# A two-layer hybrid decoder trunk on one core: side work placed by other costs, norm steps and groups of products in another order, the last norm on VectorE

## The chip, the core and the metric

The kernel runs on one core of a Trainium2 chip. Times are device microseconds of one execution, from the launch of the program on the core to its end; the metric is the median of the timed runs. TensorE multiplies matrices, VectorE, ScalarE and GpSimd work elementwise and by rows, and SyncE's queue issues most transfers.

## What is computed

For 256 tokens of width 1024 a norm, and then two layers, each of which is

```python
h = LN(ALPHA * h + mixer(h))          # ALPHA = 4 ** 0.25
h = LN(ALPHA * h + (silu(conv(gate)) * val) @ w_down)    # gate, val = split(h @ w_up)
```

The mixer projects h by one matrix into the inputs of three branches. Branch A is forgetting attention (a cumulated log gate added to the logits). Branch B is sparse attention: an indexer gives each key a score, the 64 best are kept by a top-k search, and attention runs over those. Branch C is differential attention, softmax1 - lambda * softmax2, normed per head. Queries and keys of B, C and the indexer are rotated by position. Each branch goes through its own matrix, is multiplied by a sigmoid gate of h, and the sum is projected once more.

## The kernel before

**Tiling.** The tokens are two blocks of 128 (tb 0 and 1). A norm's result h[tb][q] has 128 tokens and half of the width (q 0 and 1; the trace and the order call both "h", the order also h_90 to h_93 for h[0][0], h[0][1], h[1][0], h[1][1]). fp32 operands are split into a high and a low part, and each product is three matmuls (mm3): high by high, low by high, high by low. hTh and hTl are the transposed halves of h, which transposes on TensorE (with ident), a copy on ScalarE (hTh) and a subtraction on VectorE (hTl) make.

**Weights.** Class Stream reads all weights once, in chunks of two items of 512 columns (332 in the unit g1), by SyncE's queue into seven raw buffers. Each item is split: ScalarE copies the high half of an hl tile and VectorE (GpSimd for three items at the start) subtracts the low half. There are 16 hl buffers, so that the items split and not yet used are a reserve for TensorE. A layer has 292 items.

**The order.** The program is emitted in one sequence, and each engine works its own rows in that order. What sets the order is a planner: class Clocks keeps a clock per engine by modelled durations (cost, L195) and the time at which a tile is done. A unit of products calls Tasks.tick after every mm3; tick moves the side tasks on (generators: rotation task_rope_T, the indexer and top-k task_index, attention task_A, task_B, task_C, the merge of the branches, the MLP's activation) and calls Stream.refill, which emits a split when fewer than LOW = 3 items are in reserve, or when VectorE's clock is less than BEHIND = 1000 ns ahead of TensorE's and W.hold isn't set. A side task waits in ready (L361) until its inputs are done by these clocks. T.until ticks with idle time until a condition holds.

**Norms.** Between the halves of a layer the last products come piece by piece: for each block two halves nh of 512 columns, after each of which ln_half (L486) adds the product to h and takes its statistics; ln_tail (L545) is added as a side task, with the norm (ln_apply, L502: for each half of the width the subtraction of the mean times the gain lng, then the factor rs plus the bias lnb; rs itself is a power on GpSimd), the transposes and the splits into hTh and hTl. The next unit (unit_x_tbfirst, L573, at a layer's start, the loop of up0, L1106, in the MLP) multiplies block 0 by all its eight weight items first, and then block 1, as soon as a block's transposes are emitted (its flag). W.hold stops spare splits from the beginning of the last pieces until both tails are emitted.

**The end.** The last norm has two forms: block 0's (last_norm0, L520) by ScalarE, with gain and bias on GpSimd for one half and on VectorE for the other, and block 1's (last_norm1, L512) on VectorE; four stores of 256 KB.

## Time and profile before

| | us |
|---|---|
| timed runs | 935.35, 933.64, 935.29 (median 935.29) |
| the profiled execution's own time | 933.45 |
| its span, first to last instruction | 931.7 |
| TensorE busy | 900.1 (97%) |
| VectorE busy | 655.7 (70%) |
| ScalarE busy | 513.1 (55%) |
| GpSimd busy | 47.0 (5%) |

Every emitted instruction has the line of one helper, L242, so the profile is read by tiles and by time, not by lines. The timeline shows instructions one after the other, those alike merged (x4), with the idle time of the engine ahead of them and what ended it, in brackets. The ends of matmuls are modelled: a matmul of 512 columns shows 0.39 us, but the next begins 0.23 after it (0.12 for 256 columns); idle time that the view shows is therefore a little less than what a wait costs. The granted clock is TensorE's, 1.00 is full speed (2.4 GHz) and 0.5 half of it.

### The profile page before, as it was taken

Reading aid. Unit: us, or ns where it says so; the run is one execution under the profiler, and the core shown is the slowest. Engines: PE = TensorE matmul, PEld = TensorE weight load, DVE = VectorE, ACT = ScalarE, POOL = GpSimd, SP = SyncE. Lnnn points to the kernel's source line nnn. Section 1 sums busy time; section 2 is a strip of 40 time slices with the busy share of each in tenths; the row PEclk is TensorE's granted clock in tenths of the full one; section 3 lists DMA queues with packets and bytes.
Section 4 is the critical chain, followed back from the end, with each engine's and each line's share of the span. In section 5 each row is a group of like instructions: output and inputs, shape, how many; then the busy total and the mean of one; then the engine's idle time right before and its main releaser. Section 6 shows DMA issues by size and latency. Waiting matters only on the chain.

```text
span 931.7 us, 14406 instructions
## 1 busy us (share of the span) xinstructions
PE 900.1 (97%) x5306; PEld 787.9 (85%) x5306; DVE 655.7 (70%) x1270; ACT 513.1 (55%) x1008; POOL 47.0 (5%) x62
## 2 busy tenths in 40 slices
PE   4999999999999999999999999999999999999995
PEld 3877887888878999999888788888888799999994
DVE  7888686566678766756688957765667886766755
ACT  4753776655537655555466456765554375655540
POOL 5000010011000000000000001000110100000001
PEclk9999999999999999999999999999999999999998
DMA  8843166566526765565355322936565286566601
GB/s 307 276 141 114 48 220 236 177 200 192 189 96 227 235 196 187 181 195 182 105 185 168 113 89 72 353 115 204 186 201 176 85 295 195 178 195 188 182 3 45
DMA packets 46535, 161.45 MB, mean 173 GB/s; under 512 B 5696, under 2 KB 6208, under 8 KB 46464
## 3 DMA queue, kind: packets, MB, share of 16 engines
q1 hardware_dynamic: 44208, 154.94, 51.1%
q0 software_dynamic: 1408, 4.98, 1.6%
q8 instruction: 41, 0.67, 0.3%
q10 hardware_dynamic: 848, 0.60, 0.2%
q14 instruction: 30, 0.25, 0.1%
HBM read 159.46 MB, written 1.05 MB: 172 GB/s over the span
## 4 chain that ended last, share of the span: by engine, by line
PE 84%; DVE 9%; issue 3%; ACT 2%; DMA 1%; POOL 1%; SPq 0%; DVEq 0%; POOLq 0%; ACTq 0%
PE acc L242 52%; PE att L242 32%; DVE h L242 2%; DVE s L242 1%; DVE hl L242 1%; DVE a L242 1%; POOL rs L242 1%; DMA raw<-in_w_dram 1%; ACT a L242 1%; ACT p L242 1%; DMA lnb<-in_ln_in_b_dram 1%; DVE bst L242 1%; DVE smx L242 0%; ACT hl L242 0%; DVE t L242 0%
## 5 line engine op out<-in xcount | busy, mean ns | idle before, releaser
L242 DVE TENSOR_TENSOR hl<-raw,hl 128x512 fp32r<-128x512 f32 (+1 forms) x581 | 389.3, 695 | 185.5 <-ACT hl L242 183.9
L242 ACT ACTIVATE hl<-raw 128x512 fp32r<-128x512 f32 (+1 forms) x584 | 347.7, 624 | 192.8 <-PE att L242 92.4
L242 PE MATMUL acc<-hl,hTh 128*128 128x512 f32 (+1 forms) x896 | 285.7, 391 | 3.2 <-DVE hl L242 2.0
L242 PE MATMUL att<-hTh,hl 128*128 128x256 f32 x1280 | 231.3, 283 | 0.0
L242 PEld LDWEIGHTS att<-hTh,hl 128*128 128x128 f32 x1280 | 200.8, 192 | 1.4
L242 PEld LDWEIGHTS acc<-hl,hTh 128*128 128x128 f32 x896 | 168.3, 189 | 38.1 <-DVE hl L242 2.7
L242 PE MATMUL att<-hTl,hl 128*128 128x256 f32 x640 | 181.1, 283 | 0.0
L242 PE MATMUL acc<-hl,hTl 128*128 128x512 f32 (+1 forms) x448 | 173.4, 387 | 1.8 <-DVE hTl L242 1.8
L242 PE MATMUL acc<-hl,act 128*128 128x512 f32 x528 | 123.4, 390 | 0.0
L242 PEld LDWEIGHTS att<-hTl,hl 128*128 128x128 f32 x640 | 122.8, 192 | 0.0
L242 PEld LDWEIGHTS acc<-hl,act 128*128 128x128 f32 x528 | 97.9, 188 | 19.5
L242 PEld LDWEIGHTS acc<-hl,hTl 128*128 128x128 f32 x448 | 85.0, 190 | 17.8 <-DVE hTl L242 2.7
L242 PE MATMUL acc<-hl,oT 128*128 128x512 f32 x288 | 68.0, 391 | 0.0
L242 PEld LDWEIGHTS acc<-hl,oT 128*128 128x128 f32 x288 | 53.8, 188 | 11.0
L242 PE MATMUL acc<-hTh,hl 128*128 128x256 f32 x256 | 48.4, 289 | 3.5 <-DVE hl L242 3.5
L242 DVE SCALAR_TENSOR_TENSOR cv<-att,convp,cv 128x255 f32<-128x255 f32 x88 | 40.4, 480 | 15.4 <-ACT cv L242 13.9
L242 PE MATMUL acc<-hl,mT 128*128 128x512 f32 x192 | 45.5, 392 | 0.0
L242 PEld LDWEIGHTS acc<-hTh,hl 128*128 128x128 f32 x256 | 40.3, 192 | 5.2 <-DVE hl L242 3.9
L242 ACT ACTIVATE hTh<-att 128x512 fp32r<-128x512 f32 x16 | 9.6, 599 | 58.6 <-PE att L242 58.6
L242 PEld LDWEIGHTS acc<-hl,mT 128*128 128x128 f32 x192 | 35.6, 188 | 7.1
L242 PE MATMUL acc<-hTl,hl 128*128 128x256 f32 x128 | 36.4, 284 | 0.0
L242 POOL TENSOR_TENSOR rs<-mv,mhalf 128x1 f32<-128x1 f32 x10 | 9.1, 906 | 482.4 <-DVE mv L242 482.2
(161 smaller groups left out, 686.5 us busy)
## 6 DMA issues: line engine op xcount, KB each, us to landing
raw<-in_w_dram SPq DMA_DIRECT2D x284, 512.0 KB, 4.2
raw<-in_w_dram SPq DMA_DIRECT2D x8, 332.0 KB, 4.2
lng<-in_ln_g_dram POOLq DMA_DIRECT2D x4, 512.0 KB, 4.1
lnb<-in_ln_b_dram POOLq DMA_DIRECT2D x4, 512.0 KB, 6.4
h<-in_x_dram SPq DMA_DIRECT2D x4, 256.0 KB, 4.8
lng<-in_ln_in_g_dram SPq DMA_DIRECT2D x2, 256.0 KB, 4.9
lnb<-in_ln_in_b_dram SPq DMA_DIRECT2D x2, 256.0 KB, 5.3
wu<-in_w_ukv_dram POOLq DMA_DIRECT2D x2, 256.0 KB, 3.1
```

Of the source, the lines that this page charges most:

```text
L242: f(*args, **kw)
```

## The change

1. The planner's modelled durations are other ones, for VectorE, ScalarE's copy of an accumulated sum, table loads and GpSimd; what another engine than TensorE makes counts as done 230 ns after it, not 150, and a tile that the engine made itself isn't waited for.
2. ready also holds a side task back while the clock of its engine is more than LAG = 2500 ns ahead of TensorE's, and, on VectorE and in the projections from g1 to av, while fewer than three items are in reserve.
3. ln_apply does both subtractions and then both scalings.
4. unit_x_tbfirst and up0 take four weight items at a time (mm3_group): four matmuls high by high, four low by high, four high by low.
5. Between the halves of a layer, the last ln_half of block 1 moves into ln_tail, behind block 0's flag.
6. W.hold is set one piece later, so that one more split is emitted ahead of each norm.
7. In layer 1 the table load of ScalarE comes behind the first unit, not ahead of it.
8. The last norm is one form for both blocks, on VectorE alone, with stores of 512, 256 and 256 columns by the queues of SyncE, ScalarE and SyncE.

```diff
+LAG = 2500.0
...
-            if op == "reciprocal":
-                return 60 + 8 * n
+            if op in ("reciprocal", "bn_aggr"):
+                return 155 if op == "reciprocal" else 210
             if op == "match_replace":
-                return 140 + 1.05 * n
-            return 60 + n * (0.53 if op in ("tensor_copy", "tensor_scalar") else 1.05)
+                return 130 + 1.05 * n
+            if op == "scalar_tensor_tensor":
+                return 110 + 1.2 * n
+            if op in ("tensor_reduce", "max", "bn_stats"):
+                return 95 + 1.08 * n
+            if op == "tensor_scalar" or (op == "tensor_copy" and args[1].name[:3] not in ("att", "acc")):
+                return 150 + 0.5 * n
+            return max(160, 125 + 0.93 * n)
         if eng == "ACT":
             return 75 + 0.85 * n
-        return 630 if n <= 16 else 100 + 2.2 * n
+        return 900 if n <= 8 else 250 if n <= 32 else 100 + 2.2 * n
...
+        if op == "preload_act_table_set":
+            self.clk[eng] += 1280
+            self.table = "exp"
...
-        start = max([self.clk[eng]] + [self.done.get(x.name, 0) for x in aps[1:]])
+        start = max([self.clk[eng]] + [self.done.get(x.name, 0) for x in aps[1:] if self.by.get(x.name) != eng])
         self.clk[eng] = start + self.cost(eng, op, out, aps)
+        if "accum_out" in kw:
+            self.clk[eng] += 155
+        if eng == "ACT" and len(args) > 2 and args[2] in TABLES and TABLES[args[2]] != self.table:
+            self.table = TABLES[args[2]]
+            self.clk[eng] += 1280
         for o in outs:
-            self.done[o] = self.clk[eng] + 150
+            self.done[o] = self.clk[eng] + (150 if eng == "PE" else 230)
+            self.by[o] = eng
...
     def ready(eng, *aps):
-        while any(clocks.done.get(x.name, 0) > clocks.now(eng) - MARGIN.get(eng, 0) for x in aps):
+
+        while (any(clocks.done.get(x.name, 0) > clocks.now(eng) - MARGIN.get(eng, 0) for x in aps)
+               or clocks.clk[eng] > clocks.clk["PE"] + LAG
+               or (eng == "DVE" and l_now[0] and W.next_split - W.used < 3)):
...
     def ln_apply(tb, st, g, b):
         mu, rs = ln_stats(st)
         for q in range(2):
-            y, gq, bq = h[tb][q], g[:, 512 * q:512 * q + 512], b[:, 512 * q:512 * q + 512]
-            ve.scalar_tensor_tensor(y, y, mu, gq, ALU.subtract, ALU.mult)
-            ve.scalar_tensor_tensor(y, y, rs, bq, ALU.mult, ALU.add)
-    def store(tb, q):
-        (nc.sync, sc)[q].dma_start(out[0, tb * P:(tb + 1) * P, 512 * q:512 * q + 512], h[tb][q])
-    def last_norm1(st, g, b):
+            ve.scalar_tensor_tensor(h[tb][q], h[tb][q], mu, g[:, 512 * q:512 * q + 512], ALU.subtract, ALU.mult)
+        for q in range(2):
+            ve.scalar_tensor_tensor(h[tb][q], h[tb][q], rs, b[:, 512 * q:512 * q + 512], ALU.mult, ALU.add)
+    def last_norm(tb, st, g, b):
         mu, rs = ln_stats(st)
         for q in range(2):
-            ve.scalar_tensor_tensor(h[1][q], h[1][q], mu, g[:, 512 * q:512 * q + 512], ALU.subtract, ALU.mult)
-        for q in range(2):
-            ve.scalar_tensor_tensor(h[1][q], h[1][q], rs, b[:, 512 * q:512 * q + 512], ALU.mult, ALU.add)
-            store(1, q)
-    def last_norm0(st, g, b, half_done):
-        mu, rs = ln_stats(st)
-        nmr = small([P, 1], "nmr")
-        ve.scalar_tensor_tensor(nmr, mu, -1.0, rs, ALU.mult, ALU.mult)
-        for q in range(2):
-            sc.activation(h[0][q], h[0][q], AF.Identity, bias=nmr, scale=rs)
-        gp.tensor_tensor(h[0][0], h[0][0], g[:, 0:512], ALU.mult)
-        gp.tensor_tensor(h[0][0], h[0][0], b[:, 0:512], ALU.add)
-        while not half_done:
-            yield
-        ve.tensor_tensor(h[0][1], h[0][1], g[:, 512:1024], ALU.mult)
-        ve.tensor_tensor(h[0][1], h[0][1], b[:, 512:1024], ALU.add)
-        store(0, 1)
-        yield from ready("POOL", h[0][0])
-        nc.sync.dma_start(out[0, 0:P, 0:512], h[0][0])
+            ve.scalar_tensor_tensor(h[tb][q], h[tb][q], mu, g[:, 512 * q:512 * q + 512], ALU.subtract, ALU.mult)
+        for i, (c0, c1) in enumerate(((0, 512), (512, 768), (768, 1024))):
+            y = h[tb][c0 // 512][:, c0 % 512:c0 % 512 + c1 - c0]
+            ve.scalar_tensor_tensor(y, y, rs, b[:, c0:c1], ALU.mult, ALU.add)
+            (nc.sync, sc, nc.sync)[i].dma_start(out[0, tb * P:(tb + 1) * P, c0:c1], y)
...
-    def ln_tail(tb, st, hT, g, b, flag):
+    def ln_tail(tb, st, hT, g, b, flag, bank=None):
+        if bank is not None:
+            while 0 not in flag:
+                yield
+            ln_half(tb, 1, st, bank)
         ln_apply(tb, st, g, b)
...
+    def mm3_group(o, ls, ws, first, last):
+        n = len(ls)
+        for i, (lh, ll) in enumerate(ls):
+            mm(o, lh, ws[i][0], first and i == 0, False)
+        T.tick()
+        for i, (lh, ll) in enumerate(ls):
+            mm(o, ll, ws[i][0], False, False)
+        T.tick()
+        for i, (lh, ll) in enumerate(ls):
+            mm(o, lh, ws[i][1], False, last and i == n - 1)
+            if i % 2:
+                T.tick()
...
-            for k in range(kts):
+            for k in range(0, kts, 4):
                 if tb == 0:
-                    ws.append(W.take())
-                lh, ll = lhs(k, tb)
-                mm3(bk[tb][:, :ncols], lh, ll, ws[k][:, 0, :ncols], ws[k][:, 1, :ncols], k == 0, k == kts - 1)
+                    ws += [W.take() for _ in range(4)]
+                mm3_group(bk[tb][:, :ncols], [lhs(i, tb) for i in range(k, k + 4)],
+                          [(w[:, 0, :ncols], w[:, 1, :ncols]) for w in ws[k:k + 4]], k == 0, k + 4 == kts)
                 if tb == 1:
-                    W.free()
-                T.tick()
+                    W.free(4)
...
+        bk = unit_x_tbfirst(lhs, KD, 512, hflag)
         if l:
             sc.preload_act_table_set("natural_log_exp_and_others")
-        bk = unit_x_tbfirst(lhs, KD, 512, hflag)
         T.add(task_rope_T(evac(bk), 4, 32, 128 ** -0.5, "qbT"))
         bk = unit_x(lhs, KD, NG1)
+        l_now[0] = 1
...
+        l_now[0] = 0
...
-        W.hold = True
         hT1, flag1 = new_hT(), set()
         for tb in range(2):
             ts = slice(tb * P, (tb + 1) * P)
             st = small([P, 2, 6], "bst")
             for i, (nh, c0, c1) in enumerate(PIECES):
+                W.hold = W.hold or nh == 1
...
-                ln_half(tb, nh, st, ob[nh][tb], (c0, c1), i)
-            T.add(ln_tail(tb, st, hT1, lng, lnb, flag1))
+                if not (tb and nh):
+                    ln_half(tb, nh, st, ob[nh][tb], (c0, c1), i)
+            T.add(ln_tail(tb, st, hT1, lng, lnb, flag1, ob[1][1] if tb else None))
...
```

The order of the up0 loop is changed like that of unit_x_tbfirst, and the down projection's tail like the out projection's; the last layer calls last_norm for both blocks.

VectorE, at the norm between attention and MLP of layer 0, end of block 1 (h_92, h_93; rs is the norm's factor; an hl row is a split of the next unit's weights). Before:

```order
L242 SCALAR_TENSOR_TENSOR h_92<-h_92,mv_2753,lng_1683 128x512
L242 SCALAR_TENSOR_TENSOR h_92<-h_92,rs_2756,lnb_1684 128x512
L242 SCALAR_TENSOR_TENSOR h_93<-h_93,mv_2753,lng_1683 128x512
L242 SCALAR_TENSOR_TENSOR h_93<-h_93,rs_2756,lnb_1684 128x512
L242 TENSOR_TENSOR hl_2774<-raw_2488,hl_2774 128x512
L242 TENSOR_TENSOR hTl_2667<-att_2782,hTh_2666 128x4x128
L242 TENSOR_TENSOR hl_2789<-raw_2521,hl_2789 128x512
L242 TENSOR_TENSOR hTl_2667<-att_2795,hTh_2666 128x4x128
L242 TENSOR_TENSOR hl_2802<-raw_2521,hl_2802 128x512
```

After:

```order
L261 SCALAR_TENSOR_TENSOR h_92<-h_92,mv_2759,lng_1672 128x512
L261 SCALAR_TENSOR_TENSOR h_93<-h_93,mv_2759,lng_1672 128x512
L261 SCALAR_TENSOR_TENSOR h_92<-h_92,rs_2762,lnb_1673 128x512
L261 SCALAR_TENSOR_TENSOR h_93<-h_93,rs_2762,lnb_1673 128x512
L261 TENSOR_TENSOR hl_2780<-raw_2521,hl_2780 128x512
L261 TENSOR_TENSOR hl_2787<-raw_2521,hl_2787 128x512
L261 TENSOR_TENSOR hl_2794<-raw_2540,hl_2794 128x512
L261 TENSOR_TENSOR hTl_2667<-att_2799,hTh_2666 128x4x128
L261 TENSOR_TENSOR hTl_2667<-att_2806,hTh_2666 128x4x128
L261 TENSOR_TENSOR hl_2820<-raw_2540,hl_2820 128x512
```

Both scalings now stand behind both subtractions, and three splits stand ahead of both hTl, where one stood ahead of each.

TensorE, in the same place, from the last transposes of block 0 (h_91) into up0. Before:

```order
L242 MATMUL att_2740<-ident,h_91 128x128 x4
L242 MATMUL acc_2749<-hl_2592,hTh_2666 128x512
L242 MATMUL acc_2749<-hl_2592,hTl_2667 128x512
L242 MATMUL acc_2749<-hl_2592,hTh_2666 128x512
L242 MATMUL acc_2749<-hl_2603,hTh_2666 128x512
```

After:

```order
L261 MATMUL att_2745<-ident,h_91 128x128 x4
L261 MATMUL acc_2752<-hl_2589,hTh_2666 128x512
L261 MATMUL acc_2752<-hl_2600,hTh_2666 128x512
L261 MATMUL acc_2752<-hl_2620,hTh_2666 128x512
L261 MATMUL acc_2752<-hl_2629,hTh_2666 128x512
L261 MATMUL acc_2752<-hl_2589,hTl_2667 128x512
L261 MATMUL acc_2752<-hl_2600,hTl_2667 128x512
```

The first row that needs hTl was the second behind the transposes and is now the fifth.

VectorE, layer 1, end of the differential attention's softmax (smx a row's maximum, rina and rinv its factors; the eight SCALAR_TENSOR_TENSOR rows a<-p combine the two maps; hl rows are splits). Before:

```order
L242 RECIPROCAL rina_5675<-ssm_5753 128x2
L242 TENSOR_SCALAR a_427_5673<-a_427_5673,rina_5675 128x256 x2
L242 RECIPROCAL rinv_5676<-ssm_5758 128x2
L242 RECIPROCAL rina_5675<-ssm_5771 128x2
L242 TENSOR_SCALAR a_427_5673<-a_427_5673,rina_5675 128x256 x2
L242 RECIPROCAL rinv_5676<-ssm_5776 128x2
L242 TENSOR_SCALAR rinv_5676<-rinv_5676,nlam 128x8
L242 SCALAR_TENSOR_TENSOR a_425_5671<-p_426_5672,rinv_5676,a_425_5671 128x128 x4
L242 SCALAR_TENSOR_TENSOR a_427_5673<-p_428_5674,rinv_5676,a_427_5673 128x256 x4
L242 TENSOR_TENSOR hl_5814<-raw_5336,hl_5814 128x512
L242 TENSOR_TENSOR hl_5831<-raw_5367,hl_5831 128x512
L242 TENSOR_TENSOR hl_5846<-raw_5367,hl_5846 128x512
```

After:

```order
L261 TENSOR_TENSOR hl_5828<-raw_5427,hl_5828 128x512
L261 TENSOR_TENSOR hl_5845<-raw_5461,hl_5845 128x512
L261 RECIPROCAL rina_5667<-ssm_5804 128x2
L261 TENSOR_SCALAR a_427_5665<-a_427_5665,rina_5667 128x256 x2
L261 TENSOR_TENSOR hl_5868<-raw_5461,hl_5868 128x512
L261 TENSOR_REDUCE smx_5879<-att_5764 128x2
L261 TENSOR_TENSOR hl_5890<-raw_5529,hl_5890 128x512
L261 TENSOR_TENSOR hl_5905<-raw_5529,hl_5905 128x512
L261 RECIPROCAL rinv_5668<-ssm_5881 128x2
L261 TENSOR_SCALAR rinv_5668<-rinv_5668,nlam 128x8
L261 SCALAR_TENSOR_TENSOR a_425_5663<-p_426_5664,rinv_5668,a_425_5663 128x128 x4
L261 SCALAR_TENSOR_TENSOR a_427_5665<-p_428_5666,rinv_5668,a_427_5665 128x256 x4
```

Before, no split stands between the softmax steps; after, five do in this piece (and three more among the softmax rows ahead of it), and the eight steps stand behind them.

VectorE, the end of the program (nmr is used by ScalarE's form of the norm). Before:

```order
L242 SCALAR_TENSOR_TENSOR nmr_9229<-mv_9224,rs_9227 128x1
L242 SCALAR_TENSOR_TENSOR h_92<-h_92,acc_7577 128x512
L242 BN_STATS bst_9220<-h_92 128x6
L242 TENSOR_TENSOR h_91<-h_91,lng_7404 128x512
L242 TENSOR_TENSOR h_91<-h_91,lnb_7405 128x512
L242 SCALAR_TENSOR_TENSOR h_93<-h_93,acc_7579 128x512
L242 BN_STATS bst_9220<-h_93 128x6
```

After:

```order
L261 SCALAR_TENSOR_TENSOR h_90<-h_90,mv_9220,lng_7404 128x512
L261 SCALAR_TENSOR_TENSOR h_91<-h_91,mv_9220,lng_7404 128x512
L261 SCALAR_TENSOR_TENSOR h_90<-h_90,rs_9223,lnb_7405 128x512
L261 SCALAR_TENSOR_TENSOR h_91<-h_91,rs_9223,lnb_7405 128x256 x2
L261 SCALAR_TENSOR_TENSOR h_92<-h_92,acc_7574 128x512
L261 BN_STATS bst_9233<-h_92 128x6
L261 SCALAR_TENSOR_TENSOR h_93<-h_93,acc_7576 128x512
L261 BN_STATS bst_9233<-h_93 128x6
```

Block 0's norm is now five steps of one kind (two subtractions, three scalings), all of them ahead of block 1's first sum (h_92 with acc).

## Rows read from the trace of the kernel before

**Rows 1.** The page: busy time of each engine, its share of the span, instructions.

```profile
PE 900.1 (97%) x5306; PEld 787.9 (85%) x5306; DVE 655.7 (70%) x1270; ACT 513.1 (55%) x1008; POOL 47.0 (5%) x62
```

**Rows 2.** TensorE by stretch: length, busy (instructions), granted clock, DMA share, GB/s.

```profile
24.00:520.00 496.00, 490.62 (x2893) 1.00 0.55 178
...
571.00:574.40 3.40, 3.40 (x18) 0.50 0.78 227
```

**Rows 3.** TensorE's waits by what ended them: us in total, times, longest.

```profile
PE acc L242 <- DVE hl L242: 5.4, 3, 2.0
PE att L242 <- DVE t L242: 3.0, 3, 1.4
```

**Rows 4.** Timeline, TensorE, start: at, length, instruction [idle before, what ended it].

```profile
8.53 1.11 PE L242 MATMUL att<-ident,h 128*128 128x128 f32 x4 [8.53 <-DMA lnb<-in_ln_in_b_dram]
...
22.51 0.50 PE L242 MATMUL acc<-hl,hTh 128*128 128x512 f32 x1 [1.96 <-DVE hl L242]
```

**Rows 5.** Timeline, VectorE, start: norm of block 1 and item 6.

```profile
17.61 1.76 DVE L242 SCALAR_TENSOR_TENSOR h<-h,rs,lnb 128x512 f32<-128x512 f32 x1 [0.47 <-POOL rs L242]
...
21.76 0.70 DVE L242 TENSOR_TENSOR hl<-raw,hl 128x512 fp32r<-128x512 f32 x1
```

**Rows 6.** Timeline, GpSimd, the same stretch.

```profile
17.54 2.97 POOL L242 TENSOR_TENSOR hl<-raw,hl 128x512 fp32r<-128x512 f32 x2
```

**Rows 7.** Timeline, TensorE, layer 0: three waits in the projections.

```profile
52.79 0.41 PE L242 MATMUL att<-ident,t 128*128 128x128 f32 x2 [0.40 <-DVE t L242]
...
72.90 0.74 PE L242 MATMUL att<-ident,t 128*128 128x128 f32 x5 [1.39 <-DVE t L242]
...
119.66 0.38 PE L242 MATMUL acc<-hTh,hl 128*128 128x256 f32 x1 [1.53 <-DVE hl L242]
```

**Rows 8.** Timeline, VectorE: top-k round, rotation, last steps of differential attention.

```profile
70.30 0.61 DVE L242 MAX8 mx<-s 128x8 f32<-128x128 f32 x2
...
71.48 0.42 DVE L242 TENSOR_TENSOR ru<-t,cc 128x256 f32<-128x256 f32 x1
...
116.28 2.72 DVE L242 SCALAR_TENSOR_TENSOR a<-p,rinv,a 128x128 f32<-128x128 f32 x8
```

**Rows 9.** Timeline, TensorE, norm between attention and MLP, layer 0.

```profile
279.29 0.50 PE L242 MATMUL acc<-hl,hTl 128*128 128x512 f32 x1 [0.59 <-DVE hTl L242]
...
283.60 0.63 PE L242 MATMUL att<-ident,h 128*128 128x128 f32 x4 [0.18 <-DVE h L242]
...
285.05 0.63 PE L242 MATMUL att<-ident,h 128*128 128x128 f32 x4
```

**Rows 10.** Timeline, VectorE, the same norm: hTl of block 0, block 1.

```profile
278.56 1.27 DVE L242 TENSOR_TENSOR hTl<-att,hTh 128x512 fp32r<-128x512 f32 x2
...
282.70 0.75 DVE L242 SCALAR_TENSOR_TENSOR h<-h,rs,lnb 128x512 f32<-128x512 f32 x1 [0.45 <-POOL rs L242]
```

**Rows 11.** Timeline, TensorE, layer 1: the wait in attention.

```profile
570.48 0.38 PE L242 MATMUL acc<-hTh,hl 128*128 128x256 f32 x1 [1.93 <-DVE hl L242]
```

**Rows 12.** Timeline, VectorE and ScalarE, just before it.

```profile
569.74 2.49 DVE L242 TENSOR_TENSOR hl<-raw,hl 128x512 fp32r<-128x512 f32 x4
...
566.00 0.51 ACT L242 ACTIVATE p<-att,smx 128x256 f32<-128x256 f32 x1
...
566.45 2.22 ACT L242 ACTIVATE hl<-raw 128x512 fp32r<-128x512 f32 x4
```

**Rows 13.** Timeline, VectorE and GpSimd, the end.

```profile
922.01 1.63 DVE L242 TENSOR_TENSOR h<-h,lnb 128x512 f32<-128x512 f32 x1
923.56 0.68 DVE L242 SCALAR_TENSOR_TENSOR h<-h,acc 128x512 f32<-128x512 f32 x1
...
926.64 1.41 DVE L242 SCALAR_TENSOR_TENSOR h<-h,rs,lnb 128x512 f32<-128x512 f32 x2
...
921.50 1.59 POOL L242 TENSOR_TENSOR h<-h,lnb 128x512 f32<-128x512 f32 x1
```

**Rows 14.** Timeline, ScalarE, layer 1: the table load.

```profile
469.49 1.28 ACT L242 ACT_TABLE_LOAD   x1
```

More of the change, by code (lines that the diff above doesn't have):

```diff
@@ L192, in __init__ @@
         self.clk = dict(PE=0.0, DVE=0.0, ACT=0.0, POOL=0.0)
-        self.done, self.read = {}, {}
+        self.done, self.by, self.read = {}, {}, {}
+        self.table = "exp"
     def cost(self, eng, op, out, args):
@@ L313, in tile_hybrid @@
     uid = [0]
+    l_now = [0]
     def nm(s):
@@ L1188, in layer @@
             for i, (nh, c0, c1) in enumerate(PIECES):
+                W.hold = W.hold or nh == 1
                 for d in (NPAIR - 2, NPAIR - 1):
```

28 lines of the change are left out of this document (12 added, 16 removed).

## The prediction

> **What bounds the kernel now.** I read the page first, then TensorE's waits, then single stretches of the four engines around each wait. TensorE does something in 900.1 of the 931.7 us and VectorE in 655.7 [rows 1]. The reader is to see that almost nothing is left to win inside TensorE's own work: from 24 to 520 us it is busy 490.62 of 496 [rows 2], so whatever the change gives must come from single waits. Of the waits that the profile names, those on the low half of a weight split (tile hl) hold 5.4 us in three places, and those on t, the rotated queries and keys, 3.0 us in three places [rows 3]. Beside them stand the start (the first matmul comes at 8.53 and TensorE waits again up to 22.51 [rows 4]), the norms between the halves of a layer [rows 9, 10], and the end: VectorE's last piece and its store [rows 13]. Everything that the change does, it does at these places. In the MLP and gate stretches both orders are the same apart from a row or two, and there TensorE has no gap to lose.
>
> The sum below is made against the profiled execution, 933.45 us with a span of 931.7. The three timed runs have their median at 935.29, 1.84 above it, and their fastest at 933.64.
>
> **The start, both orders of the norm.** In block 0 (tokens 0 to 127) the two subtractions now stand ahead of the two scalings. The second subtraction needs the upper half of the gain vector, so the first transposes move from 8.53 to about 9.75: one more 0.75-us step stands ahead of them, and the half that it needs lands later (an estimate). That alone would be +0.65 at the first product, since the second transposes gain on the other side. But the start ends with a wait on VectorE up to 22.51 [rows 4], for the low half of item 6, which stands behind block 1's norm at 21.76 [rows 5]. There two steps that take 0.75 alone took 1.76 each (one stands in [rows 5], the other has the next place), beside two subtractions on GpSimd that hold 17.54 to 20.51 [rows 6]. In the new order both subtractions run before GpSimd starts, in the time that was idle (0.47 before the scaling [rows 5]), and the two scalings fall beside GpSimd instead: 17.85 + 1.76 = 19.6, and 1.0 to 1.76 more, 20.7 to 21.4. Block 1's transposes now both come after 16 matmuls and wait for that; then eight matmuls at 0.227 each and block 1 begins near 23.9, where it began before. I take +0.1, with -0.6 and +0.9 as bounds (one subtraction's idle time won; the whole late start lost).
> The Trainium skill (SBUF — State Buffer, "SBUF: two separate sides") says that a VectorE step with two inputs in SBUF and a GpSimd step that reads SBUF hold their port in turn, the second blocked for the whole instruction. [Rows 5, 6] fit that: 2.97 for two GpSimd steps and one VectorE step is about 1.1 + 0.75 + 1.1. By it the second scaling would end at 21.3, by even sharing at 20.9; the sum moves by 0.4 at most.
>
> **Side work in the projections, layer 0.** The wait before the transposes of t at 52.79 (0.40, and 0.15 of slow restart) goes: they stand nine matmuls later, 2 us, behind other products. **-0.55.** At 72.90 TensorE waited 1.39 for t [rows 7]: the rotation stands behind a round of the top-k search, 70.30 to 71.48, 1.18 [rows 8]. In the new order the index sums begin some 1.6 us earlier on VectorE (they wait for the splits no longer), the transposes stand six matmuls later (1.4 us), and two rounds instead of one stand ahead of the rotation (+1.2). 1.55 (the 1.39 and a slow restart) - 1.6 - 1.4 + 1.2 would be nothing left; as the sums also get splits between them (0.6 each, one more) I leave 0.7: **-0.8** (-1.5 to -0.1). The same place in layer 1 keeps its order of rounds: 0 (±0.5).
> At 119.66 TensorE waited 1.53 for item 56's low half [rows 7], which stood behind the eight last steps of the differential attention, 2.72 from 116.28 [rows 8]. Now splits stand between the softmax steps and ahead of the eight steps, and the transposes of a come 24 matmuls later. In return splits wait for ScalarE, whose exponentials now sit between them: I count 0.9 of small waits against 1.8. **-0.9** (-1.8 to +0.1).
>
> **The same in layer 1.** Here the wait was 1.93 up to 570.48 [rows 11]: ScalarE made its four high halves only from 566.45, after the last exponential, and VectorE the low halves from 569.74, after its eight steps [rows 12]. After it the granted clock was 0.5 from 571.0 to 574.4 [rows 2], so 1.7 of these 3.4 us were lost too. With 0.4 before it, 4.1 us in one place. The third fence of the order shows five splits among the softmax steps where none stood, with three more ahead of it, and the eight steps behind them all. What is late next: item 348 on ScalarE behind two exponentials (about 0.48 each with the sum that it reads out [rows 12]: 0.95), item 354 behind the eight steps (2.72 less the reserve of one item, 12 matmuls x 0.12 = 1.44: 1.25), and 0.4 where an exponential frees a bank late. 4.1 - 2.6 = 1.5; as these come apart, I take the clock to stay up, and **-1.9** with another 0.1 at 507 us, bounds -3.4 and -0.4.
>
> **The norms between halves.** Block 0: TensorE waited 0.59 (0.85 with its restart) for hTl at 279.29 [rows 9], since the second matmul already needs hTl, that VectorE finished at 279.8 [rows 10]. Four products with hTh now stand ahead, 4 x 0.227 = 0.91: gone. Block 1: the norm ends 0.45 earlier, since the wait for rs [rows 10] is covered by the second subtraction, but its transposes come after all 24 matmuls of block 0 and three splits (0.6 each from start to start) stand ahead of hTl, as the first fence shows. End of the norm 284.4, three splits to 286.2, hTl 286.9; TensorE's four hTh products end at about 286.1. So 0.74 on hTl, with 0.2 and 0.28 for the transposes and hTh, against 0.34 + 0.29 before (the starts at 283.60 and 285.05, set against the usual distance of 0.227 from the matmul before [rows 9]; the view shows 0.18 of the first as a gap). Net -0.26 at each of the two norms inside a layer. At the layer boundary the splits have 332 columns (0.41 each), which gives -0.75. Together **-1.27**, bounds -2.1 (no splits late) and -0.4. One further split goes ahead of each norm, beside matmuls that don't wait. The table load of 1.28 in layer 1 [rows 14] leaves the split of the first items and stands behind eight items in reserve: 0.
>
> **The end.** The 1.59 on GpSimd beside 1.63 on VectorE, and the pair like it ahead of them [rows 13], vanish, and block 0's norm is five VectorE steps done by 921.2, before TensorE's last matmul at 921.8. Then the sum of the last quarter begins at about 922.6 instead of 923.56 [rows 13] (behind the first quarter's sum and statistics, 1.4), and all that follows it is as long as before, 4.5 to the last piece. The last store is 128 KB instead of 256. **-0.9**, bounds -1.4 and -0.4. What covers block 0's steps is TensorE's last piece, 2.8 us; without it they would cost 3.0.
>
> **Sum.** 0.1 - 0.55 - 0.8 - 0.9 - 1.9 - 1.27 - 0.9 = -6.2: 927.2 against 933.45, 929.1 against the median. I give 928.5. All lower bounds together would be 922, all upper ones 932.5; independent errors make about ±2.5 of that.
>
> **Rivals.** (a) The waits only move: splits and softmax steps are the same work on VectorE, and what is put ahead of one is put behind another. Then attention keeps its waits in both layers (+2.8), the norms give nothing (+1.27), while start and end stay as reckoned: 928.5 + 4.1, about 932.5. For it: VectorE is busy for 70% of the span as it is [rows 1], and in [rows 12] both engines come late by whole groups of work. Against it: while ScalarE works through the exponentials, VectorE has nothing else queued than steps that wait for them, and that time the splits now fill. (b) The clock still falls in layer 1 after a wait of 1.25, or the other layer's wait joins it: +1.7, 930.2. (c) The change doesn't place side work where it says: the costs are still a model, a task that waits for a lagging engine can come so late that TensorE has no other work. The transposes of a come 84 matmuls later in layer 1; should the queries' stage end first, TensorE would wait up to the 2.72 of the eight steps: two layers give +5, about 933.5. (d) Slower: more and shorter waits in attention make the clock fall in several places. Each stretch of 3.4 us at 0.5 costs 1.7 [rows 2]. The forecast has none; with n of them the sum is -6.2 + 1.7 n, so four (the attention of either layer and two norms, say) bring it to nothing and from the fifth on (+2.3, 937.6) it is slower. For it: one wait of 1.93 was enough. Against it: waits of 1.39 and 1.53 at 72.9 and 119.7 were not followed by one [rows 7], as 24 to 520 us shows a granted clock of 1.00 throughout [rows 2].
>
> **How the numbers follow.** A difference of 0.2% (1.9 us) is about what a measurement of this kernel can tell from none. Forecast 926 to 930: 0.55. (b): 0.17. (a), 931.5 to 934: 0.14, of which a third is within 0.2%. (c): 0.09, most of it within. (d): 0.05, slower. So faster 0.83, same 0.12, slower 0.05. The range leaves out (d) and the far end of (c), and the best quarter of the forecast's lower bounds: 925 to 933.5.
>
> **What would show it.** Right: no wait over 1 us on t near 72 and on hl near 119 and 570; granted clock 1.00 from 20 us to the end; in block 1 of each norm a wait on hTl of 0.5 to 0.9, and none in block 0; last VectorE piece near 5.5 us after TensorE's last matmul, against 6.2. Wrong: waits on ScalarE's hl in attention of over 2 us together in a layer, a clock of 0.5 anywhere after the start, or a first product of block 1 later than 24.5.

## The result, and the profile after

The changed kernel takes 928.69 us (median of five runs, 928.38 to 929.43) against 933.64 for the kernel before, measured again beside it: ratio 0.9945, 95% interval [0.9928, 0.9962], so 3.5 to 6.7 us faster. The forecast was 928.5. The number holds; what stands behind it holds in part only, and one part of the change, the planner's new costs, works against the rest. The executions of the kernel before fall into two groups: beside the experiments 25 took 933.0 to 933.8 us with a mean granted clock of 0.995 to 0.997, and 21 took 934.6 to 935.6 with 0.993 to 0.994, so its median moves with the share of either.

The profiled execution of after took 929.43 us, its span is 927.6 (before 933.45 and 931.7). The page's busy times, which answer to [rows 1]:

```profile
PE 898.4 (97%) x5306; PEld 786.7 (85%) x5306; DVE 654.1 (71%) x1273; ACT 510.4 (55%) x1006; POOL 44.3 (5%) x60
```

TensorE's waits by what ended them (us in total, times, longest), which answer to [rows 3]:

```profile
PE att L261 <- DVE h L261: 12.7, 3, 10.7
PE att L261 <- DVE t L261: 3.4, 2, 1.8
PE acc L261 <- DVE hl L261: 2.1, 4, 0.8
PE acc L261 <- ACT hl L261: 1.7, 2, 1.2
PE acc L261 <- DVE hTl L261: 0.9, 2, 0.4
```

The waits on VectorE's hl fall from 5.4 to 2.1, those on ScalarE's grow from 1.2 to 1.7, and those on t from 3.0 to 3.4. The first line holds the start: 10.7 are the time up to the first matmul.

**Where the time went.** The two traces have the same 4656 matmuls that read weights, in nearly the same order, so the start of the n-th of them can be set side by side. By how much after is ahead of (-) or behind (+) before:

| stretch, in matmuls and us of before | after minus before at its end | in the stretch | the sum had |
|---|---|---|---|
| start, up to the 100th, 38 us | +1.15 | +1.15 | +0.1 |
| to the 200th, 70 us (t at 52 us) | +0.54 | -0.62 | -0.55 |
| to the 1000th, 265 us (t at 72, attention of layer 0) | +0.48 | -0.05 | -1.7 |
| to the 1200th, 304 us (norm) | +0.16 | -0.33 | -0.26 |
| to the 2600th, 546 us (norm, t twice) | -0.66 | -0.81 | -0.85 |
| to the 3300th, 711 us (attention of layer 1) | -2.06 | -1.41 | -1.8 |
| to the 3500th, 755 us (norm) | -2.41 | -0.35 | -0.26 |
| to the last | -2.41 | 0.00 | 0 |
| behind it: 9.83 and 8.22 us to the end of the span | -4.02 | -1.61 | -0.9 |

**The start.** The timeline of after, first VectorE (the subtraction that waits for the second half of the gain; the two scalings of block 1; [rows 5] are the like of before), then GpSimd ([rows 6]), then TensorE ([rows 4]). Columns as ahead: start, length, engine, instruction, in brackets the idle time and what ended it.

```profile
9.25 0.75 DVE L261 SCALAR_TENSOR_TENSOR h<-h,mv,lng 128x512 f32<-128x512 f32 x1 [1.61 <-DMA lng<-in_ln_in_g_dram]
...
18.00 1.41 DVE L261 SCALAR_TENSOR_TENSOR h<-h,mv,lng 128x512 f32<-128x512 f32 x2
19.32 3.45 DVE L261 SCALAR_TENSOR_TENSOR h<-h,rs,lnb 128x512 f32<-128x512 f32 x2
...
19.14 3.08 POOL L261 TENSOR_TENSOR hl<-raw,hl 128x512 fp32r<-128x512 f32 x2
```

```profile
10.72 1.97 PE L261 MATMUL att<-ident,h 128*128 128x128 f32 x8 [10.72 <-DVE h L261]
...
21.15 0.66 PE L261 MATMUL att<-ident,h 128*128 128x128 f32 x4 [0.96 <-DVE h L261]
22.82 0.66 PE L261 MATMUL att<-ident,h 128*128 128x128 f32 x4 [1.01 <-DVE h L261]
```

The second gain half landed at 9.2 here and at 8.3 in before, so of the late 1.15 about 1.0 is this execution's transfers. The rest is as reckoned: both subtractions run undisturbed, both scalings beside GpSimd, 3.45 together, near the top of what was reckoned.

**The end.** VectorE's last sum and last scalings ([rows 13] in before):

```profile
919.89 0.67 DVE L261 SCALAR_TENSOR_TENSOR h<-h,acc 128x512 f32<-128x512 f32 x1
...
922.96 1.53 DVE L261 SCALAR_TENSOR_TENSOR h<-h,rs,lnb 128x512 f32<-128x512 f32 x3
```

TensorE ends at 919.43 by its last row, and the last scaling 5.06 behind it (6.21 in before). The store then takes 3.16 to the end of the span, where it took 3.62.

### The profile page after: what moved, and what is told of

It is laid out like the page before. It is cut to its first block, busy times and chain, and to the rows that moved or that the text cites. A ratio compares the mean times of both kernels' runs of the same rounds, so it can differ in the third digit from the quotient of the medians.

```text
span 927.6 us, 14393 instructions
## 1 busy us (share of the span) xinstructions
PE 898.4 (97%) x5306; PEld 786.7 (85%) x5306; DVE 654.1 (71%) x1273; ACT 510.4 (55%) x1006; POOL 44.3 (5%) x60
## 5 line engine op out<-in xcount | busy, mean ns | idle before, releaser
L261 PE MATMUL acc<-hl,hTh 128*128 128x512 f32 (+1 forms) x896 | 276.7, 391 | 1.4 <-ACT hl L261 1.2
L261 PE MATMUL acc<-hl,hTl 128*128 128x512 f32 (+1 forms) x448 | 165.6, 387 | 0.9 <-DVE hTl L261 0.9
L261 ACT ACTIVATE t<-att 128x512 f32<-128x512 f32 (+1 forms) x32 | 18.2, 598 | 28.2 <-PE att L261 23.8
```

The source lines that it names most:

```text
L261: f(*args, **kw)
```

## The experiments

Every run was timed beside the kernel before, whose median lay between 933.6 and 934.9 in the four sessions, with the share of its two groups; so the ratio to it, given with each time, carries up to 0.14% of that. Differences in us are taken between the times themselves, unless ratios are named. Each execution's granted clock is on record: a stretch of 3.4 us at half clock costs 1.7 and lowers the mean by nearly 0.002, and where it bears on a reading it is given. "Excess" is the time between the starts of two matmuls beyond what that form usually takes (0.227 us for 512 columns, 0.120 for 256), worked out from the timelines.

**The end alone.** Edit, on the kernel before:

```diff
...
-            elif tb == 0:
-                half_done = []
-                T.add(last_norm0(st, lng, lnb, half_done))
             else:
-                last_norm1(st, lng, lnb)
+                last_norm(tb, st, lng, lnb)
```

> The kernel before with the new last norm alone (both blocks on VectorE, last store in smaller pieces). Theory: the end is worth what the two profiles differ by behind TensorE's last matmul, 9.86 against 8.17 us, so about -1.7 us against before, everything ahead of the last matmul unchanged. Rival: part of the 1.7 is an early start or a store that happened to land sooner, and the term of the sum (-0.9) was right: -0.7 to -1.0. VectorE's last piece should end 5.0 us behind TensorE's last matmul (6.2 before) by the theory.

Measured: ratio 0.9989 [0.9980, 0.9997] over twelve runs, -1.0 us (-0.3 to -1.9). In its profile 8.24 us lie behind the last matmul (9.83 before, 8.22 after), and the last scaling ends 5.07 behind it. So the trace gives 1.6, where the 1.7 expected came from rounded spans, and the timed runs 1.0, whose interval holds both. Eight of the twelve executions have a clock of 0.993 or 0.994; set against executions of the kernel before at the same clock they are 1.5 faster (933.7 against 935.2), and the three at 0.996 are 1.2 faster (932.2 against 933.4). The mechanism is shown; its size is 1.2 to 1.6 at like clock.

**The planner of before in the changed kernel.** Edit: cost, note and ready as before, all else as changed.

```diff
-               or clocks.clk[eng] > clocks.clk["PE"] + LAG
-               or (eng == "DVE" and l_now[0] and W.next_split - W.used < 3)):
+        while any(clocks.done.get(x.name, 0) > clocks.now(eng) - MARGIN.get(eng, 0) for x in aps):
...
-        return 900 if n <= 8 else 250 if n <= 32 else 100 + 2.2 * n
+        return 630 if n <= 16 else 100 + 2.2 * n
```

> The changed kernel with the planner's costs and waiting rule of before; the groups, the norm order, the hold and the new end stay. Theory: the parts add, so the norms (-1.5 in three places) and the end (-1.7) stay and the projections' and the attention's gain (-0.6 at 52 us in layer 0, -1.4 in layer 1) goes: about +2.0 against the changed kernel, with a wait of some 1.9 on hl near 570 us and the granted clock at half behind it. Rival: the groups alone shift the side work enough that the attention waits go without the new costs: within 0.5 of the changed kernel.

Measured: 925.79, ratio 0.9909 [0.9894, 0.9924]. Both theories fall: it is not slower, it is 2.9 us **faster** than the changed kernel, though the wait of layer 1 is there as foreseen, with the half clock behind it (the one execution with a clock of 0.997 took 923.37). TensorE at that wait ([rows 11] in before):

```profile
565.78 0.39 PE L245 MATMUL acc<-hTh,hl 128*128 128x256 f32 x1 [1.91 <-DVE hl L245]
```

and the stretch behind it (length, busy, granted clock, DMA share, GB/s; [rows 2] in before):

```profile
566.20:569.70 3.50, 3.50 (x19) 0.51 0.70 239
```

What it wins lies elsewhere. At the norms between halves the excess is 0.1 at each, where after has 1.2, 0.7 and 1.3; the wait near 118 us in layer 0 is gone wholly. VectorE and TensorE at the first of the norms, changed kernel:

```profile
284.61 1.89 DVE L261 TENSOR_TENSOR hl<-raw,hl 128x512 fp32r<-128x512 f32 x3
286.41 1.28 DVE L261 TENSOR_TENSOR hTl<-att,hTh 128x512 fp32r<-128x512 f32 x2
...
284.24 1.23 PE L261 MATMUL att<-ident,h 128*128 128x128 f32 x8
285.53 1.19 PE L261 MATMUL acc<-hl,hTh 128*128 128x512 f32 x4
287.15 0.96 PE L261 MATMUL acc<-hl,hTl 128*128 128x512 f32 x3 [0.43 <-DVE hTl L261]
```

and with the planner of before:

```profile
282.10 1.28 DVE L245 TENSOR_TENSOR hl<-raw,hl 128x512 fp32r<-128x512 f32 x2
283.30 0.68 DVE L245 TENSOR_TENSOR hTl<-att,hTh 128x512 fp32r<-128x512 f32 x1
283.90 0.68 DVE L245 TENSOR_TENSOR hl<-raw,hl 128x512 fp32r<-128x512 f32 x1
...
281.78 0.60 PE L245 MATMUL att<-ident,h 128*128 128x128 f32 x4
282.13 0.72 PE L245 MATMUL acc<-hl,hTh 128*128 128x512 f32 x2
282.69 0.60 PE L245 MATMUL att<-ident,h 128*128 128x128 f32 x4
```

The first transposes come ahead of the last two products of block 0 instead of behind them, and the first hTl stands behind two splits instead of three. The group's fifth matmul needs only that first hTl (it holds the first four of the eight items), so by these rows one split and two matmuls are enough to make the wait vanish.

**Without the groups.** Edit: unit_x_tbfirst and up0 item by item.

```diff
-            for k in range(0, kts, 4):
+            for k in range(kts):
...
-                mm3_group(bk[tb][:, :ncols], [lhs(i, tb) for i in range(k, k + 4)],
-                          [(w[:, 0, :ncols], w[:, 1, :ncols]) for w in ws[k:k + 4]], k == 0, k + 4 == kts)
+                mm3(bk[tb][:, :ncols], lh, ll, ws[k][:, 0, :ncols], ws[k][:, 1, :ncols], k == 0, k == kts - 1)
```

> The changed kernel with products item by item in the first unit of a layer and in up0, as before. Theory: the wait on hTl of block 0 comes back at each of three norms, 0.85 each, and the wait of block 1 (0.6 on hTl, 0.22 on hTh) shrinks, since one split and not three stands ahead of each hTl: +0.3, +0.75 and +0.3, so about +1.3 against the changed kernel. Rival: the norms' gain comes from the order of the norm steps (0.45 a block) and not from the groups: 0 to +0.3.

Measured: 927.85, ratio 0.9934 [0.9922, 0.9946]: not slower, if anything 0.8 faster, so neither the theory nor the rival's 0 to +0.3 is met. The excess at the norms is 0.9, 0.9 and 1.0 us (1.2, 0.7 and 1.3 with groups): block 0's wait on hTl is 0.30 and not 0.85, and block 1 gains as much. That the hold and the norm order are what brings block 0's hTl forward was not run apart. Under the new planner the groups are worth nothing.

**New costs, old waiting rule.** Edit: ready as before, costs as changed.

```diff
-        while (any(clocks.done.get(x.name, 0) > clocks.now(eng) - MARGIN.get(eng, 0) for x in aps)
-               or clocks.clk[eng] > clocks.clk["PE"] + LAG
-               or (eng == "DVE" and l_now[0] and W.next_split - W.used < 3)):
+        while any(clocks.done.get(x.name, 0) > clocks.now(eng) - MARGIN.get(eng, 0) for x in aps):
```

> The changed kernel with the new costs, but side work waits only for its inputs (neither for an engine that is behind nor for a reserve of three splits). Theory: the measured costs alone already place the splits among the softmax steps, so the attention of layer 1 stays within 0.5 us of the changed kernel. Rival: the two waiting rules carry it, and the splits stand behind the eight last softmax steps again: a wait of 1 to 2 us on hl in attention, +1 to +2 in all.

Measured: 932.95, ratio 0.9990 [0.9978, 1.0001]. The rival holds, and for more than it foresaw: waits on hl of 2.79 at 115.9 and 2.74 at 568.6, and near 120 us the granted clock falls as well (0.60 over 118.6 to 122.1), while behind the second wait it stays at 1.00. TensorE's two rows, and the stretches behind them:

```profile
118.63 0.39 PE L261 MATMUL acc<-hTh,hl 128*128 128x256 f32 x1 [2.79 <-DVE hl L261]
...
571.31 0.39 PE L261 MATMUL acc<-hTh,hl 128*128 128x256 f32 x1 [2.74 <-DVE hl L261]
```

```profile
118.60:122.10 3.50, 3.47 (x18) 0.60 0.65 208
...
571.00:575.00 4.00, 3.69 (x32) 1.00 0.43 144
```

Against the planner of before the two traces differ by 4.9 us between the 200th and the 1000th matmul, where this first wait lies, and by 2.9 at the three norms; elsewhere the costs win a little. The measured costs alone lose nearly all that the rest of the change wins. Which of the new costs does it was not tried.

**Old costs, new waiting rule,** the fourth corner. Edit: cost and note as before, ready as changed.

```diff
-            if op in ("reciprocal", "bn_aggr"):
-                return 155 if op == "reciprocal" else 210
+            if op == "reciprocal":
+                return 60 + 8 * n
...
-            self.done[o] = self.clk[eng] + (150 if eng == "PE" else 230)
+            self.done[o] = self.clk[eng] + 150
```

> The changed kernel with the costs of before and the new waiting rule (side work waits for engines that are behind and for a reserve of three splits): the fourth corner of costs by waiting rule. So far: both new 928.7, new costs and old rule 932.95, both old 925.8. Theory: the new rule mends what the new costs break and has little to do with the old ones, since by these VectorE's clock is rarely 2500 ns ahead: within 0.7 of both old, and the wait near 565 us in layer 1 stays. Rival: the rule is worth the same 4 us with either costs: about 922.

Measured: 925.55, ratio 0.9904 [0.9889, 0.9920]. The theory holds. The four corners, all with the new structure and end:

| | old waiting rule | new waiting rule |
|---|---|---|
| old costs | 925.79 (0.9909) | 925.55 (0.9904) |
| new costs | 932.95 (0.9990) | 928.69 (0.9945) |

The clock accounts for part of the lower row only: executions at 0.997 took 930.7 and 930.9 with the new costs and the old rule, 928.4 to 928.7 with both new, and 923.4 (a single one) with both old. So the costs lose their 7 us at like clock too, and of the 4.3 that the rule gives back about 2.3 are left; the rest is half clock that it keeps off.

**Which half of the rule.** Edit: only the wait for engines that are behind.

```diff
-               or clocks.clk[eng] > clocks.clk["PE"] + LAG
-               or (eng == "DVE" and l_now[0] and W.next_split - W.used < 3)):
+               or clocks.clk[eng] > clocks.clk["PE"] + LAG):
```

> The changed kernel without the second half of the new waiting rule: side work still waits for an engine more than 2500 ns ahead, but not for a reserve of three splits. The rule as a whole was worth 4.3 us with the new costs. Theory: the reserve carries it, since by the order the splits stand behind the eight last softmax steps again without it: about 932, with a wait of 2 to 3 us on hl near 116 and near 568 us. Rival: the lag carries it: within 1 us of the changed kernel.

Measured: 934.03, ratio 0.9995 [0.9986, 1.0004]. The theory holds: the lag alone gives nothing back, and the reserve of three splits carries it (the reserve without the lag was not run). Without it the eight last softmax steps and the splits stand as in before ([rows 8, 12]). VectorE and TensorE in layer 0, and in a fence of its own the clock of the stretch from the wait's end:

```profile
115.67 2.72 DVE L261 SCALAR_TENSOR_TENSOR a<-p,rinv,a 128x128 f32<-128x128 f32 x8
118.31 2.49 DVE L261 TENSOR_TENSOR hl<-raw,hl 128x512 fp32r<-128x512 f32 x4
...
119.05 0.58 PE L261 MATMUL acc<-hTh,hl 128*128 128x256 f32 x1 [2.77 <-DVE hl L261]
```

```profile
119.00:124.00 5.00, 4.95 (x31) 0.71 0.68 211
```

**No split ahead of hTl.** Edit, in the changed kernel:

```diff
-        if lo or reserve < self.low or (not self.hold and clk["DVE"] < clk["PE"] + BEHIND):
+        if lo or (reserve < self.low and not (self.hold and clk["PE"] > 50000)) or (not self.hold and clk["DVE"] < clk["PE"] + BEHIND):
```

> The changed kernel, in which no split at all is emitted from the last pieces of a norm until both blocks are transposed (before, fewer than three in reserve let splits through), so that hTl of block 1 stands ahead of them on VectorE. Theory: the three splits ahead of hTl are what block 1 still waits for; the 0.60 on hTl in the two norms inside a layer goes, hTh's 0.22 stays: about -1.2 against the changed kernel, if the splits now made later are still in time. Rival: the wait only moves to the first split that the next unit needs (the reserve is used up): 0 or +0.5, with waits on hl behind the norm.

Measured: 926.26, ratio 0.9910 [0.9897, 0.9924], 2.4 faster than the changed kernel at the same clock (0.997 to 0.998 in all executions of both), twice the 1.2 expected. At the norms the theory holds: 0.5 is left at each (hTh and restarts), no wait on hTl, and no later wait on a split; the traces give 0.7, 0.2 and 0.7 there. Another 0.6 was not foreseen: in layer 1's attention the third wait shrinks from 1.0 to 0.4. VectorE and TensorE at the place shown above:

```profile
284.51 1.31 DVE L261 TENSOR_TENSOR hTl<-att,hTh 128x512 fp32r<-128x512 f32 x2 [0.82 <-ACT hTh L261]
285.74 0.68 DVE L261 TENSOR_TENSOR hl<-raw,hl 128x512 fp32r<-128x512 f32 x1
...
284.53 1.20 PE L261 MATMUL acc<-hl,hTh 128*128 128x512 f32 x4
285.57 1.08 PE L261 MATMUL acc<-hl,hTl 128*128 128x512 f32 x4
```

**Groups under the old planner.** Edit: both the edits of "planner of before" and "without the groups".

```diff
-            for k in range(0, kts, 4):
+            for k in range(kts):
...
-               or clocks.clk[eng] > clocks.clk["PE"] + LAG
...
```

> The kernel with planner and waiting rule of before and items one by one (no groups); norm order, hold and end as in the changed kernel. With the old planner and groups the norms had almost no wait left (0.13 in excess at each). Theory: the groups are what covers hTl of block 0, so 0.3 comes back at each norm as without groups under the new planner, +0.9 in all against the old planner with groups (925.8). Rival: with the old planner the groups do nothing at the norms and the gain is the norm order and the hold: within 0.3. Watched besides: whether the wait of 1.69 near 118 us in layer 0, gone with the old planner and groups, comes back.

Measured: 928.78, ratio 0.9935 [0.9923, 0.9948], 3.0 slower than with groups (2.4 by the ratios). The excess at the norms is 0.65, 0.57 and 0.63 against 0.1 each: 1.6 more in all, where 0.9 was expected. The wait near 118 us comes back whole (1.69), and there is a new one of 1.12 at 46 us; on the other side no half clock follows the wait in layer 1 (1.7). So the larger half of what the groups bring under the old planner isn't the cover at the norms. That they move the ticks, and with them where splits fall in layer 0, is the likely reason; it was argued from these waits, not tested apart.

**The first norm in the order of before.** Edit, in the changed kernel's ln_apply:

```diff
             ve.scalar_tensor_tensor(h[tb][q], h[tb][q], mu, g[:, 512 * q:512 * q + 512], ALU.subtract, ALU.mult)
+            if g.tensor.name.startswith("lng0"):
+                ve.scalar_tensor_tensor(h[tb][q], h[tb][q], rs, b[:, 512 * q:512 * q + 512], ALU.mult, ALU.add)
...
```

> The changed kernel with the first norm of all (ahead of layer 0) in the order of before. Theory: the new order is worth nothing at the start (+0.1 in the sum): the difference of 1.15 us between the two profiles at the end of the first unit came from loads that landed a microsecond later in one execution, so the same within 0.5. Rival: the second gain's landing ahead of both scalings costs 0.65 and more: -0.7 to -1.2 against the changed kernel.

Measured: 930.02, ratio 0.9950 [0.9937, 0.9962] against 0.9945, but 1.3 slower than 928.69 as timed. The clock tells the two apart: the one execution at 0.998 took 928.66, within the changed kernel's 928.38 to 929.43 (0.997 to 0.998); the four others, at 0.995 to 0.996, took 929.7 to 930.4. In the profiles with the gain's second half landed at 8.2 to 8.4, the 100th product comes at 38.6 with this order and at 38.4 to 38.6 with the new one, and behind it this trace and that of the changed kernel agree within 0.1. So at like clock the order of the first norm is worth nothing; whether it moved the clock in the four is not shown.

**New planner in layer 1's projections alone,** with the strict hold:

```diff
-        l_now[0] = 1
+        l_now[0] = l
+        clocks.new = l == 1
...
+        if not self.new:
+            return self.note_old(eng, op, args, kw)
```

> Structure of the changed kernel with the strict hold; the planner's costs and rule of before everywhere but in the projections of layer 1 (from g1 to av), where the new ones hold. Theory: places add. From the old planner come layer 0's attention without its wait near 117 us (1.2) and a shorter wait for t there, from the new planner layer 1's attention without the 2.07 near 565 us and the half clock behind it (1.7): about -2 against the old planner alone (925.8), 923 to 924.5. Rival: the new planner in layer 1 starts from other clocks and other reserves, the waits come back elsewhere: 925 to 927.

Measured: 924.00, ratio 0.9888 [0.9874, 0.9901]. The theory holds, and at the norms the strict hold adds little to the planner of before (an excess of 0.1 with either): layer 0's attention keeps its 0.0, layer 1's wait is split into 0.40, 0.61 and 0.40, and its stretch has full clock. TensorE in that stretch ([rows 2] in before):

```profile
567.00:574.00 7.00, 6.39 (x49) 1.00 0.51 150
```

**Transposes of t later.** Edit, on the changed kernel with the strict hold, in the rotation task:

```diff
             yield from ready("PE", s)
+            while clocks.done.get(s.name, 0) > clocks.now("PE") - 2600.0:
+                yield
```

> The changed kernel with the strict hold, and the transposes of rotated queries and keys (t) are emitted only when the planner's clock is 2600 ns past their rotation. Theory: the waits of 1.98 and 1.70 for t (72 and 523 us) stand because the planner believes VectorE to be some 2 us earlier than it is; later transposes lose nothing, so -2.5 to -3.5 against the strict hold alone (926.3). Rival: what hangs on these transposes (softmax of branch C, its banks) comes later too, and TensorE waits there instead: -1 to +1.

Measured: 926.63, ratio 0.9913 [0.9899, 0.9926], nothing against 926.26. The rival holds (the one execution at 0.998 took 924.91, so at like clock some 1.2 may be left). The 1.98 and 1.70 on t are gone, and 1.47 near 116 us and 2.20 near 564 us stand in attention in their place, the second with a half clock behind it (0.57 over 566 to 570).

**Both together:**

```diff
...
+        clocks.new = l == 1
...
+            while clocks.done.get(s.name, 0) > clocks.now("PE") - 2600.0:
+                yield
```

> Both of the two others together: new planner in layer 1's projections alone, strict hold, later transposes of t. Theory: both gains add, 921 to 922.5. Rival: the later transposes undo in attention what they save, 923 to 925.

Measured: 922.58, ratio 0.9874 [0.9860, 0.9887], between theory and rival; it is the fastest of all, 11.8 below the kernel before by the ratio and 6.1 below the changed one (6.6 by the ratios). The same wait in layer 1 is there (2.04), but in this profile the clock stays up behind it (TensorE's row, then the stretch):

```profile
564.39 0.39 PE L300 MATMUL acc<-hTh,hl 128*128 128x256 f32 x1 [2.04 <-DVE hl L300]
```

```profile
564.00:569.00 5.00, 4.61 (x40) 1.00 0.59 198
```

## Why the prediction was right, and where it wasn't

**The start** (+0.1, measured 0 within the noise of the loads): right. The mechanism is as told; one execution's transfers moved it by a microsecond, more than the bound of +0.9 allowed for.

**Layer 0.** The wait at 52 us went (-0.62 against -0.55). The step on t at 72 failed: it grew from 1.55 to 1.97 instead of shrinking to 0.7. The prediction let the index sums begin 1.6 us earlier, because they wait for the splits no longer. In the trace they begin no earlier:

```profile
61.31 1.09 ACT L261 ACTIVATE t<-att 128x512 f32<-128x512 f32 x2 [1.07 <-PE att L261]
...
61.94 0.35 DVE L261 SCALAR_TENSOR_TENSOR s<-t,biw,m 128x128 f32<-128x128 f32 x1 [0.89 <-ACT t L261]
...
72.02 0.68 DVE L261 TENSOR_TENSOR hl<-raw,hl 128x512 fp32r<-128x512 f32 x1
72.62 0.61 DVE L261 MAX8 mx<-s 128x8 f32<-128x128 f32 x2
...
73.80 0.41 DVE L261 TENSOR_TENSOR ru<-t,cc 128x256 f32<-128x256 f32 x1
...
75.22 1.06 PE L261 MATMUL att<-ident,t 128*128 128x128 f32 x8 [1.81 <-DVE t L261]
```

ScalarE waits for TensorE's scores there, which no place in ScalarE's own queue brings forward: 61.94 less the 0.54 by which the whole program is late is the 61.4 of before. The other terms came as reckoned: a split (0.60) and the second round of the top-k (1.18) stand ahead of the rotation, and the transposes come six matmuls later (1.36). 1.55 + 0.60 + 1.18 - 1.36 is the 1.97 measured. In attention 0.75 and 0.51 of waits replaced 1.69 and small ones: -0.5 where -0.9 was taken.

**Layer 1's attention** (-1.8 or -1.9 with the clock, measured -1.41 with the stretch around it): right in mechanism. The three waits named are there: on splits behind two exponentials (0.63 in excess, ended by ScalarE's half, and 0.61, ended by VectorE's; 0.95 reckoned), on the split behind the eight steps (1.0, 1.25 reckoned), on a bank (0.26, 0.4 reckoned). These came to 2.5 where 2.6 was reckoned. But the sum took 1.9 for the place, of which 0.1 is for 507 us, while its own terms, 4.1 - 2.6, give 1.5: the 0.3 between has no row, and the trace bears out the 1.5. TensorE of after, and the clock of the stretch with the first two:

```profile
569.61 0.39 PE L261 MATMUL acc<-hTh,hl 128*128 128x256 f32 x1 [0.47 <-ACT hl L261]
570.34 0.39 PE L261 MATMUL acc<-hTh,hl 128*128 128x256 f32 x1 [0.34 <-DVE hl L261]
...
580.08 0.39 PE L261 MATMUL acc<-hTh,hl 128*128 128x256 f32 x1 [0.84 <-DVE hl L261]
```

```profile
569.00:574.00 5.00, 4.18 (x33) 1.00 0.54 186
```

The wait for t at 525 us grew by 0.3, within its bounds.

**The norms** (-1.27; measured -0.33, -0.86 and -0.35, -1.54): right, and by the steps told: nothing on block 0, 0.60 on hTl (0.74) and 0.22 on hTh (0.28) of block 1, behind three splits; at the layer boundary no wait on hTl. That these were the price was shown by taking them away (the strict hold). How the gain divides between the norm order, the sum moved into ln_tail and the later hold was not run apart, nor was the table load's new place.

**The end** (-0.9; 1.6 in the profiles, 1.0 timed alone and 1.2 to 1.5 at like clock): mechanism right, the term undersized. VectorE was done with block 0's norm 0.8 before TensorE's last matmul and so added the last quarter 0.46 behind it, where 0.76 was reckoned from the two sums in a row; and the smaller last store gave 0.46, though the earlier sum alone (923.56 to 922.6) already fills the 0.9.

So the sum of -6.2 came out as -4.0 between the two profiles, with a microsecond lost to late loads, and as -4.95 between the medians: two misses in layer 0 (1.7) and one in layer 1 (0.4) against an undersized end (0.7) and norms (0.3). That 928.5 lies 0.2 from the median is luck in good part: the sum gave 927.2 or 929.1 by the reference taken, and 927.4 against the 933.64 measured beside the change.

Of the signs named for right, the clock, the waits on hl in attention (0.84 at most) and block 0 of the norms came true; the wait on t at 75 us did not (1.81). One sign of wrong came: block 1's first product stands at 25.16, not by 24.5. It is the execution with the late loads; with the gain half at 8.26 (the profile of the strict hold) it stands at 24.17.

What the forecast didn't see is that the change's first part is its dear one. The terms were read from the order of the changed kernel as a whole, and the gain in attention was put down to where side work stands; the four corners show that the measured costs alone cost 7 us, that the rule on the reserve gives 4 of them back, and that structure and end alone would have been 2.9 faster. In none of the rivals did the planner's costs lose by themselves: (c) came nearest, but it feared tasks held back too long, not splits that come late. (a), waits that move behind other splits, is in part what happened at the norms and on t.

Rival (d), more stretches of half clock: none in the changed kernel (0.997 to 0.998 in all five executions), two in the profile with new costs and the lag alone (near 120 and 576 us; 0.994 to 0.996 in its executions), which is also the slowest. It was a real danger, and the reserve is what kept it off. Open is why a wait of some 2 us is followed by a half clock in some profiles (the kernel before, the old planner, later transposes of t with the new one) and not in others (2.04 in the fastest kernel, 1.91 and 1.92 in the two without groups). It is not the program alone: with new costs and the old rule one wait of 2.79 was followed by it and one of 2.74 was not, in the same execution, and the twelve executions of that kernel have clocks of 0.990 to 0.997 and times of 937.4 to 930.7. The two groups of the kernel before are 1.66 us apart, and their mean clocks (0.9953 and 0.9935) differ by 0.0018, over the span 1.7 us, what one more stretch of half clock costs; where it lies isn't on record.

## What to carry to other kernels

When a planner sets an order, put its costs, its waiting rules and the code's structure on trial apart: here better costs alone made the order worse, since they delayed the spare work that kept TensorE's reserve, and a rule on the reserve itself (no fewer than three, and none ahead of a critical step) did, under these costs, what they were thought to do. Read the wait at each place as the race of one queue's rows: one split and two matmuls decided 0.6 us at the two norms inside a layer. Read the clock of every execution beside its time, since a profile shows one of them. And a step that stands earlier in its queue gains nothing while it waits for another engine; look first at what released it.

## What the runs showed of the hardware

Two VectorE steps with both inputs in SBUF beside two GpSimd steps took 3.42 to 3.46 us together in all eleven profiles of the new order, where two such steps take 1.41 alone. The granted clock did not fall behind every wait of 2 us: 0.51 behind one of 1.91, 1.00 behind one of 2.04, and in one execution 0.60 behind one of 2.79 and 1.00 behind one of 2.74. Executions of one kernel differ in it: 0.995 to 0.997 at 933.0 to 933.8 us, 0.993 to 0.994 at 934.6 to 935.6. The second gain half, the last load that the first norm's subtractions wait for, landed at 7.35 to 9.23 us in the fourteen profiles, 1.9 apart.
